# Seven block products in place of eight for some row-block pairs, in chunk pairs, with the heads first, in a one-core encoder block

## The chip, the cores and the metric

The kernel runs on one core of a Trainium2 chip. The metric is the device time of one execution in microseconds. TensorE is called PE, VectorE DVE, ScalarE ACT, GpSimd POOL and SyncE SP, as the profile calls them.

## What is computed

One layer of a hybrid encoder block on 256 tokens of width 2048, all in float32. `D_FF` is 5632; there are 8 retention heads with 256 columns of q and k and 512 of v and g each.

```python
h = rms_norm(x, g_mix)
cb, cc, cv, q, k, v, g, gate_conv, gate_ret = split(h @ w_in)          # 22528 columns
y_conv = (cb * causal_dwconv3(cc * cv)) @ w_conv_out
o = head_group_norm(retention(rotary(q), rotary(k), v), g_ret)
y_ret = (silu(g) * o) @ w_ret_out                                      # 4096 rows
x = x + (sigmoid(gate_conv) * y_conv + sigmoid(gate_ret) * y_ret) @ w_o
a, b = split(rms_norm(x, g_ffn) @ w_ffn_in)                            # 2 x 5632 columns
x = x + (silu(a) * b) @ w_ffn_out
x = x + sigmoid(rms_norm(x, g_ple) @ w_ple_gate) * (p @ w_ple_proj)
out = rms_norm(x, g_final)
```

## The kernel before

Every product of activations and weights goes through `project` (L204). Its output is one chunk of 512 columns (`W`) for the two token tiles of 128 rows, one PSUM bank each. The weights of a chunk are loaded in pieces of four row blocks of 128 rows (`KG`, 1 MB, four `raw` buffers, queue of SP). The float32 product is made of three products of fp32r parts: `split` (L184) copies two row blocks, 1024 columns, to the high part on ACT (L191) and subtracts on DVE to the low part (L192); `products` (L195) then issues, for each row block and token tile, high by high (L200), low weights by high (L201) and high weights by low (L202). The low and high parts of weights have three buffers each (`split_pool`). A row block thus costs 2 x 3 matmuls with 128x128 stationary and 512 moving columns, a chunk of 16 row blocks 96.

The activations stand transposed, features on partitions, as pairs of high and low parts: `transposed_split` (L145) turns a chunk by eight PE transposes (L137) into PSUM, from where ACT (L152 or, with a gain, L159) and DVE (L153 or L160) take the parts. Such steps are put off by `later` (L99) until so many `group_done` (L102) have passed, that is, pieces of four row blocks of the stream.

The order is: cc, cv, cb chunk by chunk with the short convolution (`conv_u`, `conv_gate`), then gc, gr and the convolution's output `co`, then the eight heads (qk, v, g each), the retention's output `ro`, `wo`, the feed-forward chunks fa and fb in turn, `fo` over all 44 row blocks, and the embedding with the last norm (pg, pp). The results of a chunk are read by ACT or DVE straight from PSUM. `project` has a pool of four banks (`ps_mm`), transposes, scores and the heads' outputs another of four (`ps_aux`). The instructions stand on each engine in an order that the tile scheduler sets when the program is built; each engine works through its own queue in that order, and an instruction that waits holds all behind it.

## Time and profile before

| | us |
|---|---|
| median of 3 runs | 2219.84 |
| lowest and highest | 2218.95, 2222.67 |
| span of the profiled execution | 2220.6 |
| PE busy, share of the span | 2205.8, 99% |
| DVE busy | 1222.5, 55% |
| ACT busy | 975.4, 44% |
| DMA queue q1, share of 16 engines | 55.2% |

The page gives no time of its own for the profiled execution beside its span, which lies 0.8 us above the median; so the sums below are made against 2220.6. A matmul's duration in a row (389 ns) is longer than its share of PE's time, since the matmuls are pipelined: the pace is read from the distance of their starts. A mean duration on DVE or ACT likewise overlaps the next operation by a little.

### The profile page before, as it was taken

The page shows a single profiled execution, that of the slowest core. Times are in us where ns is not written, and L with a number is a line of the kernel's source. Part 1 is how long each engine was busy: PE and PEld are TensorE (multiplying, and loading weights), DVE is VectorE, ACT ScalarE, POOL GpSimd, SP SyncE. Part 2 cuts the span into 40 slices and gives each one's busy share as a digit, 9 for nine tenths or more (in the row PEclk, how much of TensorE's full clock was granted, in tenths as well). Part 3 has the DMA queues.
Part 4 walks back from the last instruction along what each step waited for, and adds up shares of the span by engine and source line. Part 5 has one row for each costly group of instructions (what it writes and reads, how often), then busy time and mean ns, then how long its engine had stood idle before and what let it go on. Part 6 is the DMA issues. An engine that isn't in the chain of part 4 may idle for free.

```text
span 2220.6 us, 24771 instructions
## 1 busy us (share of the span) xinstructions
PE 2205.8 (99%) x10054; PEld 1834.0 (83%) x10054; DVE 1222.5 (55%) x1347; ACT 975.4 (44%) x1101; POOL 9.4 (0%) x19
## 2 busy tenths in 40 slices
...
GB/s 263 187 189 190 189 189 190 195 199 193 174 190 182 181 179 186 178 178 180 177 190 189 190 209 205 185 190 192 191 184 191 191 190 183 196 194 191 191 195 128
DMA packets 229106, 420.05 MB, mean 189 GB/s; under 512 B 7424, under 2 KB 42368, under 8 KB 228992
## 3 DMA queue, kind: packets, MB, share of 16 engines
q1 hardware_dynamic: 228992, 418.48, 55.2%
q8 instruction: 78, 1.28, 0.2%
...
## 4 chain that ended last, share of the span: by engine, by line
PE 99%; DMA 0%; ACT 0%; issue 0%; DVE 0%; SPq 0%; ACTq 0%; POOLq 0%
PE fo_ps L201 4%; PE fa_ps L202 4%; PE fa_ps L201 4%; PE fa_ps L200 4%; PE fo_ps L202 4%; PE fb_ps L200 4%; PE fo_ps L200 4%; PE fb_ps L202 4%; PE fb_ps L201 4%; PE v_ps L202 3%; PE v_ps L201 3%; PE v_ps L200 3%; PE g_ps L202 3%; PE g_ps L201 3%; PE g_ps L200 3%; PE qk_ps L201 3%
## 5 line engine op out<-in xcount | busy, mean ns | idle before, releaser
L192 DVE TENSOR_TENSOR fo_lo<-fo_raw,fo_hi 128x1024 fp32r<-128x1024 f32 x88 | 107.8, 1225 | 123.5 <-ACT fo_hi L191 123.5
L192 DVE TENSOR_TENSOR fa_lo<-fa_raw,fa_hi 128x1024 fp32r<-128x1024 f32 x88 | 107.8, 1225 | 111.4 <-ACT fa_hi L191 111.4
L192 DVE TENSOR_TENSOR fb_lo<-fb_raw,fb_hi 128x1024 fp32r<-128x1024 f32 x88 | 107.8, 1225 | 110.8 <-ACT fb_hi L191 110.8
L191 ACT CAST fa_hi<-fa_raw 128x1024 fp32r<-128x1024 f32 x88 | 92.8, 1054 | 142.8 <-PE fa_ps L202 87.9
L191 ACT CAST fo_hi<-fo_raw 128x1024 fp32r<-128x1024 f32 x88 | 92.8, 1055 | 137.4 <-PE fo_ps L202 132.4
L191 ACT CAST fb_hi<-fb_raw 128x1024 fp32r<-128x1024 f32 x88 | 92.7, 1053 | 121.9 <-PE fb_ps L202 85.3
L201 PE MATMUL fo_ps<-fo_lo,aT_hi 128*128 128x512 f32 x352 | 137.1, 389 | 0.0
L202 PE MATMUL fa_ps<-fa_hi,h2T_lo 128*128 128x512 f32 x352 | 137.0, 389 | 0.0
L201 PE MATMUL fa_ps<-fa_lo,h2T_hi 128*128 128x512 f32 x352 | 137.0, 389 | 0.0
L202 PE MATMUL fo_ps<-fo_hi,aT_lo 128*128 128x512 f32 x352 | 137.0, 389 | 0.0
L201 PE MATMUL fb_ps<-fb_lo,h2T_hi 128*128 128x512 f32 x352 | 136.9, 389 | 0.0
L202 PE MATMUL fb_ps<-fb_hi,h2T_lo 128*128 128x512 f32 x352 | 136.9, 389 | 0.0
L200 PE MATMUL fa_ps<-fa_hi,h2T_hi 128*128 128x512 f32 x352 | 127.2, 392 | 0.0
L200 PE MATMUL fo_ps<-fo_hi,aT_hi 128*128 128x512 f32 x352 | 124.4, 390 | 0.0
L192 DVE TENSOR_TENSOR ro_lo<-ro_raw,ro_hi 128x1024 fp32r<-128x1024 f32 x64 | 78.4, 1225 | 83.0 <-ACT ro_hi L191 83.0
L200 PE MATMUL fb_ps<-fb_hi,h2T_hi 128*128 128x512 f32 x352 | 122.6, 389 | 0.0
L191 ACT CAST g_hi<-g_raw 128x1024 fp32r<-128x1024 f32 x64 | 67.2, 1050 | 109.8 <-PE g_ps L202 81.9
L191 ACT CAST v_hi<-v_raw 128x1024 fp32r<-128x1024 f32 x64 | 67.4, 1054 | 106.3 <-PE v_ps L202 53.3
L192 DVE TENSOR_TENSOR v_lo<-v_raw,v_hi 128x1024 fp32r<-128x1024 f32 x64 | 78.3, 1224 | 62.4 <-ACT v_hi L191 62.4
L191 ACT CAST ro_hi<-ro_raw 128x1024 fp32r<-128x1024 f32 x64 | 67.5, 1054 | 102.3 <-PE ro_ps L202 98.9
L192 DVE TENSOR_TENSOR qk_lo<-qk_raw,qk_hi 128x1024 fp32r<-128x1024 f32 x64 | 78.3, 1224 | 61.0 <-ACT qk_hi L191 61.0
L192 DVE TENSOR_TENSOR g_lo<-g_raw,g_hi 128x1024 fp32r<-128x1024 f32 x64 | 78.3, 1224 | 60.4 <-ACT g_hi L191 60.4
...
## 6 DMA issues: line engine op xcount, KB each, us to landing
fa_raw<-in_w_ffn_in_dram SPq DMA_DIRECT2D x44, 1024.0 KB, 4.9
fb_raw<-in_w_ffn_in_dram SPq DMA_DIRECT2D x44, 1024.0 KB, 4.9
fo_raw<-in_w_ffn_out_dram SPq DMA_DIRECT2D x44, 1024.0 KB, 5.0
...
v_raw<-in_w_in_dram SPq DMA_DIRECT2D x32, 1024.0 KB, 5.0
g_raw<-in_w_in_dram SPq DMA_DIRECT2D x32, 1024.0 KB, 4.8
ro_raw<-in_w_ret_out_dram SPq DMA_DIRECT2D x32, 1024.0 KB, 5.0
cv_raw<-in_w_in_dram SPq DMA_DIRECT2D x16, 1024.0 KB, 4.9
```

What stands on the lines that cost most here:

```text
L191: last_copy[0] = nc.scalar.copy(out=hi, in_=raw[:, h0 : h0 + 2, :])
L192: nc.vector.tensor_tensor(out=lo, in0=raw[:, h0 : h0 + 2, :], in1=hi.bitcast(F32), op=ALU.subtract)
L200: nc.tensor.matmul(out=ps, lhsT=xh[:, ts], rhs=wh, start=first, stop=False)
L201: nc.tensor.matmul(out=ps, lhsT=xh[:, ts], rhs=wl, start=False, stop=False)
L202: nc.tensor.matmul(out=ps, lhsT=xl[:, ts], rhs=wh, start=False, stop=last)
```

## The change

Outside the heads, the retention's output and the embedding, chunks go in pairs. `product_group` takes two chunks of 512 columns at once, and row blocks in pairs, so that a step is a product of 2 x 2 blocks: two token tiles by two row blocks, and two row blocks by two chunks. Where the table `FAST3` or `FAST4` has True for a row-block pair (three or four of eight), the step has seven block products in place of eight, from sums and differences of the blocks: of the activations, made once by `further_forms` on DVE and ACT, and of the weights, made for each step by four DVE operations of 512 columns on the loaded piece (L260 to L263 of the changed kernel), after the parts of three of the four loaded blocks were taken and before the parts of the four combinations are. The products are accumulated in seven, at the end four, PSUM banks, and put together by one ACT copy and four DVE additions after the last such pair (L288 to L292) and four additions at the end (L297). The other pairs keep eight products, in a form that fits these sums.

`halves` replaces `split`: one ACT copy and one DVE subtraction over up to 2048 columns. One pool, `part`, of six buffers holds these parts, two buffers at each call; `raw` has three buffers, and one pool of eight PSUM banks serves all. `blk` has 30 in place of 36 buffers. Five heads come first, then the first half of the retention's output, which is put into DRAM (`acc`), the other three heads, the convolution with the second half of the retention's output after its first chunk, the gates, `co`, `wo`, and the feed-forward: after each chunk `f` from the third on, parts of the output product `fo` over two chunks' rows follow. In a head, g comes before qk and v.

```diff
...
+NBLK = 30
+FAST3 = (False, True, False, True, False, True, False, False)
+FAST4 = (False, True, False, True, True, False, True, False)
...
-    blk_pool = ctx.enter_context(tc.tile_pool(name="blk", bufs=36))
-    raw_pool = ctx.enter_context(tc.tile_pool(name="raw", bufs=4))
-    split_pool = ctx.enter_context(tc.tile_pool(name="split", bufs=3))
     small = ctx.enter_context(tc.tile_pool(name="small", bufs=2))
-    ps_mm = ctx.enter_context(tc.tile_pool(name="ps_mm", bufs=4, space=PSUM))
-    ps_aux = ctx.enter_context(tc.tile_pool(name="ps_aux", bufs=4, space=PSUM))
+    blk_pool = ctx.enter_context(tc.tile_pool(name="blk", bufs=NBLK))
+    diff_pool = ctx.enter_context(tc.tile_pool(name="diff", bufs=4))
+    raw_pool = ctx.enter_context(tc.tile_pool(name="raw", bufs=3))
+    part_pool = ctx.enter_context(tc.tile_pool(name="part", bufs=6))
+    ps_pool = ctx.enter_context(tc.tile_pool(name="ps", bufs=8, space=PSUM))
+    dram_pool = ctx.enter_context(tc.tile_pool(name="dram", bufs=1, space=bass.MemoryType.DRAM))
...
+    t1, t2 = slice(0, P), slice(P, 2 * P)
+    def further_forms(hi, lo, forms, fast, name):
+        stt = nc.vector.scalar_tensor_tensor
+        tt = nc.vector.tensor_tensor
+        for j0 in range(0, hi.shape[1], 2):
+            i = len(forms)
+            if not any(fast[i:]):
+                forms.append(None)
+                continue
+            js = slice(j0, j0 + 2)
+            a = small.tile([P, 2, S], F32, tag="form_a", name=f"{name}_a", bufs=1)
+            tt(out=a, in0=hi[:, js, :].bitcast(F32), in1=lo[:, js, :].bitcast(F32), op=ALU.add)
+            n = 4 if fast[i] else 2
+            mix = small.tile([P, 4, P], F32, tag="form_m", name=f"{name}_m", bufs=1)[:, :n, :]
+            if fast[i]:
+                a11, a12, a21, a22 = a[:, 0, t1], a[:, 1, t1], a[:, 0, t2], a[:, 1, t2]
+                stt(out=mix[:, 0, :], in0=a21, scalar=-1.0, in1=a22, op0=ALU.mult, op1=ALU.subtract)
+                stt(out=mix[:, 1, :], in0=mix[:, 0, :], scalar=-1.0, in1=a11, op0=ALU.mult, op1=ALU.subtract)
+                tt(out=mix[:, 2, :], in0=a11, in1=a21, op=ALU.subtract)
+                tt(out=mix[:, 3, :], in0=a12, in1=mix[:, 1, :], op=ALU.subtract)
+                more = blk([P, 2, 4, P], F32R, f"{name}_s")
+            else:
+                tt(out=mix, in0=a[:, :, t1], in1=a[:, :, t2], op=ALU.subtract)
+                more = diff_pool.tile([P, 2, 2, P], F32R, tag="diff", name=f"{name}_d")
+            nc.scalar.copy(out=more[:, 0], in_=mix)
+            tt(out=more[:, 1], in0=mix, in1=more[:, 0].bitcast(F32), op=ALU.subtract)
+            forms.append([(more[:, 0, k, :], more[:, 1, k, :]) for k in range(n)])
...
+    def product_group(lhs, forms, fast, w, c1, c2, name):
+        last_fast = max(i for i, f in enumerate(fast) if f)
+        left = {p: 0 for p in range(1, 9)}
+        for i, f in enumerate(fast):
+            for p in (1, 2, 3, 4, 5, 6, 7) if f else (2, 4, 3, 5) if i < last_fast else (2, 4, 3, 8):
+                left[p] += 1 if f else 2
+        total, banks = dict(left), {}
+        def add(p, stat, mov):
+            if p not in banks:
+                banks[p] = bank(f"{name}_p{p}")
+            thrice(banks[p], stat, mov, left[p] == total[p], left[p] == 1)
+            left[p] -= 1
+        tt = nc.vector.tensor_tensor
+        ca = blk([P, NT, W], F32, f"{name}_ca")
+        cb = blk([P, NT, W], F32, f"{name}_cb")
+        for i, f in enumerate(fast):
+            rows = w[2 * i * P : 2 * (i + 1) * P, :].rearrange("(c p) n -> p c n", p=P)
+            raw = raw_pool.tile([P, 4, W], F32, tag="raw", name=f"{name}_raw{i}")
+            nc.sync.dma_start(out=raw[:, 1:3, :], in_=rows[:, :, c1 : c1 + W])
+            nc.sync.dma_start(out=raw[:, 0:4:3, :], in_=rows[:, :, c2 : c2 + W])
+            blocks = lhs[2 * i : 2 * i + 2]
+            (a11, a21), (a12, a22) = ([(h[:, t], l[:, t]) for t in (t1, t2)] for h, l in blocks)
+            if f:
+                b11, b21, b22 = halves(raw[:, 1:4, :], f"{name}_b{i}")
+                tt(out=raw[:, 1, :], in0=raw[:, 1, :], in1=raw[:, 0, :], op=ALU.subtract)
+                tt(out=raw[:, 0, :], in0=raw[:, 3, :], in1=raw[:, 0, :], op=ALU.subtract)
+                tt(out=raw[:, 3, :], in0=raw[:, 3, :], in1=raw[:, 1, :], op=ALU.add)
+                tt(out=raw[:, 2, :], in0=raw[:, 2, :], in1=raw[:, 3, :], op=ALU.subtract)
+                t3, tt1, t4, tt2 = halves(raw, f"{name}_t{i}")
+                s1, s2, s3, s4 = forms[i]
+                for p, stat, mov in (
+                    (1, a11, b11),
+                    (2, a12, b21),
+                    (3, s4, b22),
+                    (7, s3, t3),
+                    (6, s2, tt2),
+                    (5, s1, tt1),
+                    (4, a22, t4),
+                ):
+                    add(p, stat, mov)
+            else:
+                b12, b11, b21, b22 = halves(raw, f"{name}_b{i}")
+                for j, (x1, x2, b1, b2) in enumerate(((a11, a21, b11, b12), (a12, a22, b21, b22))):
+                    add(2, x1, b1)
+                    add(4, x2, b1)
+                    if i < last_fast:
+                        add(5, x2, b2)
+                        add(3, forms[i][j], b2)
+                    else:
+                        add(3, x1, b2)
+                        add(8, x2, b2)
+            if i == last_fast:
+                nc.scalar.copy(out=ca[:, 0, :], in_=banks[1])
+                tt(out=cb[:, 0, :], in0=banks[6], in1=ca[:, 0, :], op=ALU.add)
+                tt(out=ca[:, 1, :], in0=banks[7], in1=cb[:, 0, :], op=ALU.add)
+                tt(out=cb[:, 1, :], in0=banks[5], in1=ca[:, 1, :], op=ALU.add)
+                tt(out=cb[:, 0, :], in0=banks[5], in1=cb[:, 0, :], op=ALU.add)
+            if i < len(fast) - 1:
+                group_done()
+        for p, c, t in ((2, ca, 0), (4, ca, 1), (3, cb, 0), (8, cb, 1)):
+            if p in banks:
+                tt(out=c[:, t, :], in0=banks[p], in1=c[:, t, :], op=ALU.add)
+        group_done()
+        return ca, cb
...
+    def halves(src, name):
+        n = src.shape[1]
+        hi, lo = (part_pool.tile([P, 4, W], F32R, tag="part", name=f"{name}_{x}") for x in ("hi", "lo"))
+        last_copy[0] = nc.scalar.copy(out=hi[:, :n, :], in_=src)
+        nc.vector.tensor_tensor(out=lo[:, :n, :], in0=src, in1=hi[:, :n, :].bitcast(F32), op=ALU.subtract)
+        return [(hi[:, j, :], lo[:, j, :]) for j in range(n)]
...
+    head(0, first)
+    for h in range(1, HEADS // 2):
+        head(h)
+    head(4)
+    ret_out(0)
+    for h in range(5, HEADS):
+        head(h, gate_last=h == HEADS - 1)
...
+    def conv_cv(n):
+        c, v = product_group(hT, hF, FAST3, w_in[0], C_C + n * W, C_V + n * W, f"cv{n}")
         for t in range(NT):
+            nc.scalar.activation(out=c[:, t, :], in_=c[:, t, :], func=AF.Copy, scale=r1[t])
             nc.vector.scalar_tensor_tensor(
+                out=v[:, t, :], in0=v[:, t, :], scalar=r1[t], in1=c[:, t, :], op0=ALU.mult, op1=ALU.mult
             )
+        uT = small.tile([P, 4, S + 2], F32, tag="uT", name=f"uT{n}", bufs=1)
+        ys[n] = blk([P, 4, S], F32, f"y{n}")
+        later(2, partial(conv_u, n, v, uT, ys[n]))
+    def conv_b(n):
+        bs = product_group(hT, hF, FAST3, w_in[0], C_B + n * W, C_B + (n + 1) * W, f"cb{n}")
+        for i, b in enumerate(bs):
+            for t in range(NT):
+                nc.scalar.activation(out=b[:, t, :], in_=b[:, t, :], func=AF.Copy, scale=r1[t])
+            later(2 + i, partial(conv_gate, n + i, b, ys[n + i]))
+    conv_cv(0)
+    ret_out(1)
+    conv_cv(1)
+    conv_b(0)
+    conv_cv(2)
+    conv_cv(3)
+    conv_b(2)
...
+    for n in range(0, D // W, 2):
+        ms = product_group(ycT, ycF, FAST3, w_conv_out[0], n * W, (n + 1) * W, f"co{n}")
+        for i, m in enumerate(ms):
+            gc, gr = gates[n + i]
+            nc.vector.tensor_tensor(out=m, in0=m, in1=gc, op=ALU.mult)
+            nc.vector.tensor_tensor(out=m, in0=m, in1=gr, op=ALU.add)
+            later(2 + i, partial(turn_m, n + i, m))
...
+    def ffn_in(n):
+        a, b = product_group(h2T, h2F, FAST4, w_ffn_in[0], n * W, D_FF + n * W, f"f{n}")
+        r2 = scale2[0] = scale2[0] or rows2.done()
         sa = blk([P, NT, W], F32, f"sa{n}")
         for t in range(NT):
+            nc.scalar.activation(out=sa[:, t, :], in_=a[:, t, :], func=AF.Sigmoid, scale=r2[t])
             nc.vector.scalar_tensor_tensor(
+                out=a[:, t, :], in0=a[:, t, :], scalar=r2[t], in1=sa[:, t, :], op0=ALU.mult, op1=ALU.mult
             )
+            nc.vector.scalar_tensor_tensor(
+                out=a[:, t, :], in0=b[:, t, :], scalar=r2[t], in1=a[:, t, :], op0=ALU.mult, op1=ALU.mult
+            )
+        later(2, partial(turn_a, n, a))
...
+    for n in range(NF):
+        ffn_in(n)
+        if n >= 2:
+            part = (n // 2 - 1) * 2
+            for c in (0, 1) if n % 2 == 0 and n < NF - 1 else (2, 3) if n % 2 else ():
+                ffn_out((part, part + 1), c)
+    for c in range(D // W):
+        ffn_out((NF - 3, NF - 2, NF - 1), c, last=True)
...
```

The first place is DVE's queue in the feed-forward, at chunk 5. Before, in chunk fb5, each row is the low part of two row blocks, with two products of the chunk fa5 between:

```order
L192 TENSOR_TENSOR fb5_lo0_11559<-fb5_raw_11556,fb5_hi0_11558 128x1024
L192 TENSOR_TENSOR fb5_lo2_11563<-fb5_raw_11556,fb5_hi2_11562 128x1024
L554 SCALAR_TENSOR_TENSOR sa5_11549<-fa5_ps0_11395,r2_r_9219,sa5_11549 128x512
L554 SCALAR_TENSOR_TENSOR sa5_11549<-fa5_ps1_11396,r2_r_9219,sa5_11549 128x512
L192 TENSOR_TENSOR fb5_lo0_11593<-fb5_raw_11590,fb5_hi0_11592 128x1024
L192 TENSOR_TENSOR fb5_lo2_11597<-fb5_raw_11590,fb5_hi2_11596 128x1024
L192 TENSOR_TENSOR fb5_lo0_11627<-fb5_raw_11624,fb5_hi0_11626 128x1024
L192 TENSOR_TENSOR fb5_lo2_11631<-fb5_raw_11624,fb5_hi2_11630 128x1024
```

Now, at the row-block pairs 3 and 4 of chunk f5, both with seven products (`b` are parts of loaded blocks, `t` parts of combinations):

```order
L329 TENSOR_TENSOR f5_b3_lo_11783<-f5_raw3_11779,f5_b3_hi_11782 128x1536
L260 TENSOR_TENSOR f5_raw3_11779<-f5_raw3_11779 128x512
L261 TENSOR_TENSOR f5_raw3_11779<-f5_raw3_11779 128x512
L262 TENSOR_TENSOR f5_raw3_11779<-f5_raw3_11779 128x512
L263 TENSOR_TENSOR f5_raw3_11779<-f5_raw3_11779 128x512
L329 TENSOR_TENSOR f5_t3_lo_11791<-f5_raw3_11779,f5_t3_hi_11790 128x2048
L329 TENSOR_TENSOR f5_b4_lo_11819<-f5_raw4_11815,f5_b4_hi_11818 128x1536
L260 TENSOR_TENSOR f5_raw4_11815<-f5_raw4_11815 128x512
L261 TENSOR_TENSOR f5_raw4_11815<-f5_raw4_11815 128x512
L262 TENSOR_TENSOR f5_raw4_11815<-f5_raw4_11815 128x512
L263 TENSOR_TENSOR f5_raw4_11815<-f5_raw4_11815 128x512
L329 TENSOR_TENSOR f5_t4_lo_11827<-f5_raw4_11815,f5_t4_hi_11826 128x2048
```

Between the low part `b3_lo` and the low part `t3_lo` now stand four operations on the loaded piece, each of which waits for DVE's own count, and the next pair's `b4_lo` comes only after `t3_lo`. On ACT's queue the copies stand in the order `b3_hi`, `t3_hi`, `b4_hi`, `t4_hi`: `t3_hi` reads the piece `f5_raw3` that the four operations wrote, and `b4_hi` stands behind it.

The second place is PE's queue at the same chunk. Before, for one row block of fb5, three products for each token tile:

```order
L200 MATMUL fb5_ps0_11554<-fb5_hi0_11558,h2T0_hi_9417 128x512
L201 MATMUL fb5_ps0_11554<-fb5_lo0_11559,h2T0_hi_9417 128x512
L202 MATMUL fb5_ps0_11554<-fb5_hi0_11558,h2T0_lo_9418 128x512
L200 MATMUL fb5_ps1_11555<-fb5_hi0_11558,h2T0_hi_9417 128x512
L201 MATMUL fb5_ps1_11555<-fb5_lo0_11559,h2T0_hi_9417 128x512
L202 MATMUL fb5_ps1_11555<-fb5_hi0_11558,h2T0_lo_9418 128x512
```

And now, from the products with `t3` to the first with `b4`'s low part:

```order
L227 MATMUL f5_p7_11734<-f5_t3_hi_11790,h2T1_s_9461 128x512
L227 MATMUL f5_p6_11738<-f5_t3_hi_11790,h2T1_s_9461 128x512
L227 MATMUL f5_p5_11689<-f5_t3_hi_11790,h2T1_s_9461 128x512
L227 MATMUL f5_p4_11685<-f5_t3_hi_11790,h2T1_hi_9427 128x512
L227 MATMUL f5_p1_11724<-f5_b4_hi_11818,h2T2_hi_9727 128x512
L227 MATMUL f5_p2_11681<-f5_b4_hi_11818,h2T2_hi_9727 128x512
L227 MATMUL f5_p3_11693<-f5_b4_hi_11818,h2T2_s_9754 128x512
L228 MATMUL f5_p7_11734<-f5_t3_lo_11791,h2T1_s_9461 128x512
L229 MATMUL f5_p7_11734<-f5_t3_hi_11790,h2T1_s_9461 128x512
L228 MATMUL f5_p6_11738<-f5_t3_lo_11791,h2T1_s_9461 128x512
L229 MATMUL f5_p6_11738<-f5_t3_hi_11790,h2T1_s_9461 128x512
L228 MATMUL f5_p5_11689<-f5_t3_lo_11791,h2T1_s_9461 128x512
```

Four products with `t3_hi` and three with `b4_hi` stand ahead of those that need `t3_lo`; all of b4's others stand behind these. The third place is DVE's queue in the convolution. Before, the taps of chunk 1 (`y1`, L326 and L331) stood between two low parts:

```order
L192 TENSOR_TENSOR cb1_lo0_1092<-cb1_raw_1089,cb1_hi0_1091 128x1024
L326 TENSOR_SCALAR y1_993<-uT1_992,gains_76 128x256 x4
L331 SCALAR_TENSOR_TENSOR y1_993<-uT1_992,gains_76,y1_993 128x256 x6
L192 TENSOR_TENSOR cb1_lo2_1096<-cb1_raw_1089,cb1_hi2_1095 128x1024
L331 SCALAR_TENSOR_TENSOR y1_993<-uT1_992,gains_76,y1_993 128x256 x2
L192 TENSOR_TENSOR cb1_lo0_1126<-cb1_raw_1123,cb1_hi0_1125 128x1024
```

Now the taps (L649) stand between the four operations on the piece `cb0_raw3`:

```order
L329 TENSOR_TENSOR cb0_b3_lo_5936<-cb0_raw3_5932,cb0_b3_hi_5935 128x1536
L649 SCALAR_TENSOR_TENSOR y1_5799<-uT1_5798,gains_78,y1_5799 128x256 x2
L260 TENSOR_TENSOR cb0_raw3_5932<-cb0_raw3_5932 128x512
L649 SCALAR_TENSOR_TENSOR y1_5799<-uT1_5798,gains_78,y1_5799 128x256 x4
L261 TENSOR_TENSOR cb0_raw3_5932<-cb0_raw3_5932 128x512
L649 SCALAR_TENSOR_TENSOR y1_5799<-uT1_5798,gains_78,y1_5799 128x256 x2
L262 TENSOR_TENSOR cb0_raw3_5932<-cb0_raw3_5932 128x512
L640 MEMSET uT2_6433 128x4x2
L263 TENSOR_TENSOR cb0_raw3_5932<-cb0_raw3_5932 128x512
L329 TENSOR_TENSOR cb0_t3_lo_5944<-cb0_raw3_5932,cb0_t3_hi_5943 128x2048
L329 TENSOR_TENSOR cb0_b4_lo_5972<-cb0_raw4_5968,cb0_b4_hi_5971 128x2048
```

There other work separates the four operations, and none stands between L263 and `cb0_t3_lo`.

In the whole program PE has 10054 matmuls before and 9796 after, DVE 1347 and 1707 instructions, ACT 1066 and 842. In 16 of the 86 steps with seven products something else stands on DVE's queue between L263 and the low part of the combinations, in 70 nothing.

## Rows read from the trace of the kernel before

**Rows 1.** The page: span, busy time of each engine, and the chain that ended last.

```profile
span 2220.6 us, 24771 instructions
PE 2205.8 (99%) x10054; PEld 1834.0 (83%) x10054; DVE 1222.5 (55%) x1347; ACT 975.4 (44%) x1101; POOL 9.4 (0%) x19
PE 99%; DMA 0%; ACT 0%; issue 0%; DVE 0%; SPq 0%; ACTq 0%; POOLq 0%
```

**Rows 2.** Windows of convolution, heads, feed-forward: length, PE, PEld, DVE, ACT, POOL, PEclk, DMA, GB/s.

```profile
60.00:545.00 485.00, 485.00 (x2173) 402.27 (x2172) 249.39 (x257) 212.46 (x222) 0.00 (x0) 1.00 0.56 191
545.00:1129.00 584.00, 584.00 (x2679) 484.75 (x2678) 366.47 (x464) 254.93 (x287) 5.52 (x8) 1.00 0.54 181
1390.00:1870.00 480.00, 480.00 (x2160) 398.34 (x2159) 254.62 (x238) 205.91 (x215) 0.00 (x0) 1.00 0.55 189
```

**Rows 3.** Chain in order of time (start, length, engine): transposes, and matmuls 96 apart.

```profile
64.73 0.87 PE uT L137 x8
436.38 0.45 PE gr_ps L200 x2
458.13 0.45 PE co_ps L200 x2
```

**Rows 4.** Groups by line and shape, DVE: busy us, mean ns, idle before and releaser.

```profile
L192 DVE TENSOR_TENSOR fa_lo<-fa_raw,fa_hi 128x1024 fp32r<-128x1024 f32 x88 | 107.8, 1225 | 111.4 <-ACT fa_hi L191 111.4
L331 DVE SCALAR_TENSOR_TENSOR y<-uT,gains,y 128x256 f32<-128x256 f32 x32 | 13.3, 479 | 0.0
L520 DVE TENSOR_TENSOR m<-m,co 128x512 f32<-128x512 f32 x8 | 5.1, 682 | 0.0
L160 DVE SCALAR_TENSOR_TENSOR h2T_lo<-h2T_t,gains,h2T_hi 128x256 fp32r<-128x256 f32 x16 | 7.0, 478 | 0.6 <-ACT h2T_hi L159 0.2
L589 DVE TENSOR_TENSOR x<-x,x 128x256 f32<-128x256 f32 x4 | 1.7, 425 | 0.1
```

**Rows 5.** Timeline of DVE, independent operations back to back: start, length.

```profile
1154.72 1.28 DVE L519 TENSOR_TENSOR m<-ro_ps,gr 128x512 f32<-128x512 f32 x2
1155.92 1.28 DVE L520 TENSOR_TENSOR m<-m,co 128x512 f32<-128x512 f32 x2
1157.12 1.22 DVE L192 TENSOR_TENSOR ro_lo<-ro_raw,ro_hi 128x1024 fp32r<-128x1024 f32 x1
```

**Rows 6.** Timeline of DVE, operations that read what the one before wrote (L589 after L588).

```profile
2199.52 0.42 DVE L588 TENSOR_TENSOR x<-pp_ps,x 128x256 f32<-128x256 f32 x1 [3.10 <-ACT x L587]
2199.98 0.42 DVE L589 TENSOR_TENSOR x<-x,x 128x256 f32<-128x256 f32 x1
2200.32 0.42 DVE L588 TENSOR_TENSOR x<-pp_ps,x 128x256 f32<-128x256 f32 x1
```

**Rows 7.** Groups by line and shape, ACT: the same columns as rows 4.

```profile
L191 ACT CAST fa_hi<-fa_raw 128x1024 fp32r<-128x1024 f32 x88 | 92.8, 1054 | 142.8 <-PE fa_ps L202 87.9 <-PE fb_ps L202 50.0 <-PE wo_ps L202 4.9
L347 ACT CAST ych<-y 128x512 fp32r<-128x512 f32 x8 | 4.9, 622 | 0.4
```

**Rows 8.** Timeline, from ACT's copy to the DVE operation that waits for it.

```profile
1501.42 1.05 ACT L191 CAST fb_hi<-fb_raw 128x1024 fp32r<-128x1024 f32 x1 [1.67 <-PE fb_ps L202]
1502.51 1.22 DVE L192 TENSOR_TENSOR fb_lo<-fb_raw,fb_hi 128x1024 fp32r<-128x1024 f32 x1 [1.49 <-ACT fb_hi L191]
```

**Rows 9.** Waits of PE: engine, line, waited for; us, times, longest.

```profile
PE cc_ps L200 <- ACT hT_hi L159: 4.2, 1, 4.2
```

**Rows 10.** Windows at the start, columns as in rows 2: TensorE's clock around that wait.

```profile
4.00:8.00 4.00, 2.15 (x14) 1.63 (x12) 0.17 (x1) 0.00 (x0) 0.00 (x0) 1.00 0.90 295
8.00:12.00 4.00, 1.68 (x4) 1.21 (x5) 2.08 (x4) 3.14 (x6) 0.00 (x0) 0.52 1.02 373
12.00:16.00 4.00, 4.00 (x16) 3.43 (x16) 2.73 (x5) 2.27 (x6) 0.00 (x0) 0.62 1.05 392
16.00:20.00 4.00, 4.00 (x19) 3.27 (x19) 3.22 (x5) 2.48 (x4) 0.00 (x0) 1.00 1.03 378
```

**Rows 11.** The page's DMA issues (KB each, us to landing) and the queue's share.

```profile
q1 hardware_dynamic: 228992, 418.48, 55.2%
fa_raw<-in_w_ffn_in_dram SPq DMA_DIRECT2D x44, 1024.0 KB, 4.9
```

305 lines of the change are left out of this document (168 added, 137 removed).

## The prediction

> **What bounds the kernel now.** I read the page's shares and its chain first: PE is busy for 99% of the span and the whole chain is PE, while DVE has 55% and ACT 44% [rows 1]. An average can hide a stage, so the windows come next: in the convolution, the heads and the feed-forward PE is busy in every microsecond at full clock, and DVE has 249 of 485, 366 of 584 and 255 of 480 us [rows 2]. The kernel is a PE stream from end to end. Its pace is read from the chain: two first matmuls of pieces that lie 96 matmuls apart start at 436.38 and 458.13, so one costs 21.75 / 96 = 0.2266 us; eight transposes cost 0.87 [rows 3]. The DMA queue is at 55%, and a piece of 1 MB lands in 4.9 us [rows 11]; both kernels load the same weights, and a `raw` buffer comes free whole pairs (5 us each) before it is needed, so I put no cost on transfers. PE waits only once for ACT, for 4.2 us at the start [rows 9].
>
> **What is taken from PE.** A step with seven products drops one of eight block products, three matmuls. The FAST3 groups are 14 (4 cv, 2 cb, 4 gate, 2 co, 2 wo) with 3 such steps, the FAST4 groups 11 with 4: 42 + 44 = 86 steps, 258 matmuls, as the order counts (10054 to 9796). At 0.2266 that is 58.5 us. If PE stayed the bound, the time would be 2162 us. So all depends on whether DVE and ACT can feed it.
>
> **What one step costs on DVE.** Durations of shapes that the trace lacks come from its shapes: on DVE 1024 elements take 1225 ns and 512 take 682 [rows 4], 1.06 ns per element, so I estimate 1.77 us for 1536 and 2.31 for 2048. Independent operations start 0.08 before the one before ends (pairs of 512 at 1154.72, 1155.92, 1157.12, so 0.60 each) [rows 5], so a 2048 one occupies 2.23. Operations that wait for the one before start 0.04 after its end (0.46 from start to start for 0.42 of work, against 0.34 without the wait) [rows 6], so each of the four operations L260 to L263, which all wait for DVE's own count, takes 0.68 + 0.04 = 0.72; the lower bound is 0.60. On ACT 1024 take 1054 ns and 512 take 622 [rows 7], 0.844 ns per element, so a 2048 copy takes 1.92; from its end to the DVE operation that needs it pass 0.04 [rows 8].
>
> The order has DVE do, for one such step, `b_lo` (1.77 + 0.04), the four operations (2.88), then `t_lo`, which waits for ACT's copy `t_hi`, which waits for L263. In 70 of 86 steps nothing stands between, so DVE stands still for 0.04 + 1.92 + 0.04 = 2.0 us; then `t_lo` 2.23. Sum 8.92 us. PE has for the same step 21 x 0.2266 = 4.76 us. An ordinary step is the reverse: DVE 2.23, PE 24 x 0.2266 = 5.44. The closing eight additions of a group (L289 to L297) are 8 x about 0.64 = 5.1 us more on DVE. `b_hi` of the next step stands behind `t_hi` on ACT, and `b_lo` behind `t_lo` on DVE, so no buffer can shorten this: DVE's queue runs step after step, and PE can only use up what was made ahead.
>
> **Stages with FAST3.** DVE per group: 3 x 8.92 + 5 x 2.23 + 5.1 = 43.0. PE: 183 matmuls, 41.5; before, 2 x 21.75 = 43.5. So DVE already passes PE, and all other work on DVE falls on the path. I count it by the operations, with 0.40 for 256 elements, 0.60 to 0.68 for 512 and 1.14 for two of 512 less the overlap [rows 4, 5]: the forms of the activations (13 with seven products at 0.68 + 4 x 0.33 + 0.68 = 2.7, 12 others at 0.68 + 2 x 0.4 = 1.45) 52; L682 8 x 0.67 = 5; taps 32 x 0.40 = 13; L664 and L666 16 x 0.60 = 10; the products with the gates 16 x 1.14 = 18; low parts of mT and h2T 8 x 0.60 and 16 x 0.42 = 12; what head 7 leaves, 9. That is 119. Off it go 20, for the 16 standstills in which such work lies (1.3 each), and 10 beside the second half of the retention's output, where all steps are ordinary and DVE has time to spare. The stage comes to 14 x 43.0 + 119 - 30 = 691. Before, the same products and 16 sets of transposes took 28 x 21.75 + 16 x 0.87 = 623. **Cost 68 us.**
>
> **The feed-forward.** From the third chunk on, two parts of `fo` (96 ordinary matmuls) follow each group. PE's time for such a period is (180 + 96) x 0.2266 + 0.87 = 63.4, DVE's 4 x 8.92 + 4 x 2.23 + 5.1 + 3.9 for the products with r2 and aT + 4 x 2.23 for `fo` = 62.5. They are even, so what counts is the order within the period: steps 3 and 4 are neighbours and take 2 x (8.92 - 4.76) = 8.3 more of DVE than of PE, while what is made ahead of them in six buffers is one step, about 4.7: PE stands for about 3.7 there, and for 1.45 at step 6 (4.2 less the 2.7 won in step 5). Period 68.5; before 288 x 0.2266 + 0.87 = 66.1; over 9 periods +22. The first two chunks have no `fo` behind: DVE 4 x 8.92 + 4 x 2.23 + 5.1 + 3.9 = 53.6, before 43.5 + 0.87 = 44.4, so 9.2 x 2 = +18. **Cost 40 us.**
>
> **What costs nothing.** Heads, retention output and embedding keep 24 matmuls for 2.23 of DVE per two row blocks, and DVE had 366 of 584 us in the heads [rows 2]; the merged copies leave that sum as it was (two of 1225 against one of 2.31) and the different order of heads and convolution moves PE work only. The trips of the retention sum through DRAM are a few pieces among 218 MB and are not read until stages later. Sum: 2220.6 + 68 + 40 = 2328.6, set against the span 2220.6, 0.8 above the median; I say **2328**.
>
> **A rule against the merging.** The row shows a 1024 copy on ACT at 1.05 and the DVE operation behind it 0.04 later [rows 7, 8]; with 2048 elements the first DVE operation can't start before all four blocks are copied. The Trainium skill, "Perfetto Trace Analysis", section Optimizing Scalar/DVE Operations, advises to break up instructions that cause bubbles on other engines. By it, halves would make the standstill about 1.1 instead of 2.0 and the sum some 86 x 0.9 = 77 us smaller at most; the kernel does the opposite, so my sum keeps the 2.0.
>
> **Rivals.**
> *A, faster: PE stays the bound.* With s for DVE's time per step, the FAST3 stage takes 14 x (3 x s + 16.3) + 89 us (11.2 and 5.1 in each group, 119 - 30 beside), as long as this is over PE's 595. At s = 7.3 it is 623, what it was, and the feed-forward then has about 20 us of PE's gain: 2200. Without the standstill s is 6.92, the stage 607, the time about 2175; at 6.6 all is PE's, 2162. For it: DVE's busy time after, 1222 + 86 x 4.4 (a 1536 low part and four operations, less the merging) + 25 x 5.1 + 60 of forms, is about 1790 of 2162 us, under PE's; and where DVE is ahead its standstill hides. Against it: 2.0 of the 8.92 is a wait whose two ends the order shows, and in the FAST3 groups there is no slack to be ahead with. The skill page named, section Identifying the Most-Contended Engine, takes the engine with the highest occupancy as the bottleneck; by that PE still is, and the time 2162. In the trace of before the rule held [rows 1]. Chance 0.10.
>
> *B, far slower: the clock falls.* After PE's one wait the granted clock was 0.52 and 0.62 over 8 us, which is the 1.2 GHz level for most of them, and 1.00 again from 16 us on [rows 10]. If the waits of 1.5 to 4 us in the groups did the same, the 1.2 GHz level over 4 to 8 us, that is 3 to 6 us more in each of 25 groups, would put 75 to 150 on top: 2405 to 2480. Against it: most stalls here are split over a step, PE working between. Chance 0.09.
>
> *C, near no change, 2216 to 2250:* s between 7.7 and 8.1, as with the four operations at 0.60 (s = 8.44) and some of the standstills filled besides. Chance 0.05, of which 0.03 within 0.2%.
>
> *That it doesn't do what it says* is excluded by the count of matmuls in the order.
>
> **The range.** Low: four operations at 0.60 give 86 x 4 x 0.12 = -41; the stalls of the feed-forward taken up by the reserve give -25; holes filled, -12: 2250. High: the PE transposes, which stand in PE's queue and wait for DVE's sums of the group before, at 1.5 us in 25 groups, +38; short falls of the clock [rows 10], +40: 2405. Within lies 0.76, the rest being A, B and C. About 0.2% is what measurement can tell from no change here; faster by more than it has 0.10, within it 0.03, slower 0.87.
>
> **What would show it.** Right: DVE waits for ACT at the line of `t_lo`, about 2 us each, 70 times or more; PE waits for parts of weights, its share falls to about 92% with the chain passing through DVE and ACT; FAST3 groups last 47 to 50 us, feed-forward periods about 68, the first two chunks about 53; DVE is busy about 1790 us. Wrong: PE at 98% and more without such waits (A); L260 to L263 clearly under 0.68 apart; PEclk under 1.00 over whole stages (B); or PE waiting for DMA, which my sum has at nothing.

## The result, and the profile after

The changed kernel takes 2330.26 us (median of 4 runs, 2326.76 to 2332.11) against 2219.39 before: a ratio of 1.0491, 95% interval 1.0477 to 1.0506. It is slower, by 111 us, and 2 us from the time that was forecast. The page of the profiled execution, three lines that answer to [rows 1]:

```profile
span 2329.7 us, 24877 instructions
PE 2214.4 (95%) x9796; PEld 1803.6 (77%) x9796; DVE 1710.1 (73%) x1707; ACT 1048.8 (45%) x877; POOL 10.2 (0%) x19
PE 67%; DVE 17%; ACT 6%; issue 5%; DMA 3%; SPq 0%; ACTq 0%; DVEq 0%; POOLq 0%
```

PE lost its 258 matmuls and is busy for 9 us more than before; the chain, all PE before, now goes through DVE and ACT for 23%. Windows by stage show where (columns as in [rows 2]): cv of chunk 0; the second half of the retention's output (from 721.5 to 809.5); the rest of the stages with FAST3; the feed-forward.

```profile
669.20:718.00 48.80, 43.30 (x177) 33.50 (x176) 40.84 (x48) 23.85 (x23) 0.00 (x0) 0.93 0.43 148
718.00:810.50 92.50, 92.50 (x414) 76.69 (x413) 50.96 (x42) 35.27 (x25) 0.00 (x0) 1.00 0.69 231
810.50:1434.40 623.90, 578.00 (x2481) 457.97 (x2479) 532.10 (x543) 306.36 (x252) 0.00 (x0) 0.98 0.54 183
1434.40:2220.20 785.80, 738.53 (x3168) 597.51 (x3169) 633.86 (x599) 359.05 (x276) 1.47 (x1) 0.96 0.52 177
```

Apart from the start and the end, only the stages with seven products have a PE that is not busy all the time, and in the last two of these windows DVE has 85% and 81%. Measured from the first matmul of a stage to the first of the next, and without the 87.9 us of the retention's output between: the stages with FAST3 take 677 us where the same products took 625; the feed-forward 786 where it took 732; heads, retention output and start 757 for 754; the embedding 109.5 for 109.7. The loss is 52 + 54 + 3.5.

What DVE waits for, of the rows with a `t_lo` (us in all, times, longest):

```profile
DVE f_t_lo L329 <- ACT f_t_hi L328: 85.6, 42, 2.1
DVE gate_t_lo L329 <- ACT gate_t_hi L328: 19.9, 10, 2.6
DVE cv_t_lo L329 <- ACT cv_t_hi L328: 19.2, 10, 2.1
DVE cb_t_lo L329 <- ACT cb_t_hi L328: 12.1, 6, 2.1
DVE wo_t_lo L329 <- ACT wo_t_hi L328: 11.0, 5, 3.4
DVE co_t_lo L329 <- ACT co_t_hi L328: 8.5, 5, 2.1
```

78 waits of 2.0 us, 156 us in all. In the stages with FAST3 these are 71 us beside 573 of DVE's busy time, of 673 us; in the feed-forward 86 beside 634, of 786. So a DVE that is busy for 81% to 85% has a queue with little room left. And what PE waits for, which answers to [rows 9], the first rows:

```profile
PE f_p L227 <- ACT f_t_hi L328: 38.1, 15, 3.4
PE cv_p L227 <- ACT cv_t_hi L328: 8.1, 5, 3.2
PE co_p L227 <- ACT co_t_hi L328: 6.6, 4, 2.9
```

One step with seven products on DVE, pair 3 of a chunk f and the beginning of pair 4 (timeline: start, length; in brackets idle time and releaser):

```profile
1698.86 1.75 DVE L329 TENSOR_TENSOR f_b_lo<-f_raw,f_b_hi 128x1536 fp32r<-128x1536 f32 x1
1700.65 0.69 DVE L260 TENSOR_TENSOR f_raw<-f_raw 128x512 f32<-128x512 f32 x1
1701.37 0.69 DVE L261 TENSOR_TENSOR f_raw<-f_raw 128x512 f32<-128x512 f32 x1
1702.10 0.69 DVE L262 TENSOR_TENSOR f_raw<-f_raw 128x512 f32<-128x512 f32 x1
1702.82 0.69 DVE L263 TENSOR_TENSOR f_raw<-f_raw 128x512 f32<-128x512 f32 x1
1705.57 2.29 DVE L329 TENSOR_TENSOR f_t_lo<-f_raw,f_t_hi 128x2048 fp32r<-128x2048 f32 x1 [2.05 <-ACT f_t_hi L328]
1707.78 1.75 DVE L329 TENSOR_TENSOR f_b_lo<-f_raw,f_b_hi 128x1536 fp32r<-128x1536 f32 x1
```

From `b_lo` to `b_lo` are 8.92 us, the four operations start 0.72 apart, the standstill is 2.05: the term on which the prediction's sum rests, to the hundredth. PE meets it one step later:

```profile
1711.46 0.39 PE L229 MATMUL f_p<-f_b_hi,h2T_s 128*128 128x512 f32 x1
1714.50 1.65 PE L227 MATMUL f_p<-f_t_hi,h2T_s 128*128 128x512 f32 x3 [2.65 <-ACT f_t_hi L328]
1715.94 0.63 PE L227 MATMUL f_p<-f_t_hi,h2T_hi 128*128 128x512 f32 x1
1716.37 0.73 PE L227 MATMUL f_p<-f_b_hi,h2T_hi 128*128 128x512 f32 x1
1718.21 0.40 PE L229 MATMUL f_p<-f_t_hi,h2T_s 128*128 128x512 f32 x1
```

It stands for 2.65 us, and the matmuls behind take 0.63 in place of 0.39, for some 3 us: the granted clock has fallen (0.83 in the windows under "Zeros in the stall").

### The profile page after: what moved, and what is told of

The parts are those of the page before. It is cut to its first block, busy times and chain, and to the rows that moved or that the text cites. A ratio compares the mean times of both kernels' runs of the same rounds, so it can differ in the third digit from the quotient of the medians.

```text
span 2329.7 us, 24877 instructions
## 1 busy us (share of the span) xinstructions
PE 2214.4 (95%) x9796; PEld 1803.6 (77%) x9796; DVE 1710.1 (73%) x1707; ACT 1048.8 (45%) x877; POOL 10.2 (0%) x19
## 3 DMA queue, kind: packets, MB, share of 16 engines
q1 hardware_dynamic: 235008, 426.88, 54.4%
## 4 chain that ended last, share of the span: by engine, by line
PE 67%; DVE 17%; ACT 6%; issue 5%; DMA 3%; SPq 0%; ACTq 0%; DVEq 0%; POOLq 0%
PE f_p L227 3%; PE f_p L228 3%; PE f_p L229 3%; PE fo_ps L350 3%; PE fo_ps L348 3%; PE fo_ps L349 3%; PE g_ps L348 3%; PE g_ps L349 3%; PE g_ps L350 3%; DVE f_b_lo L329 3%; PE v_ps L350 2%; PE ro_ps L229 2%; PE ro_ps L228 2%; PE qk_ps L350 2%; PE qk_ps L348 2%
## 5 line engine op out<-in xcount | busy, mean ns | idle before, releaser
L329 DVE TENSOR_TENSOR f_b_lo<-f_raw,f_b_hi 128x2048 fp32r<-128x2048 f32 (+1 forms) x88 | 176.1, 2020 | 20.8 <-ACT f_b_hi L328 20.6
L328 ACT CAST f_b_hi<-f_raw 128x2048 fp32r<-128x2048 f32 (+1 forms) x88 | 147.6, 1692 | 54.4 <-PE fo_ps L349 27.3
L329 DVE TENSOR_TENSOR f_t_lo<-f_raw,f_t_hi 128x2048 fp32r<-128x2048 f32 x44 | 100.9, 2292 | 85.6 <-ACT f_t_hi L328 85.6
L228 PE MATMUL f_p<-f_b_lo,h2T_hi 128*128 128x512 f32 x374 | 146.0, 390 | 0.0
L229 PE MATMUL f_p<-f_b_hi,h2T_lo 128*128 128x512 f32 x374 | 145.6, 389 | 0.0
L227 PE MATMUL f_p<-f_b_hi,h2T_hi 128*128 128x512 f32 x374 | 138.3, 407 | 6.3 <-ACT f_b_hi L328 4.6
L329 DVE TENSOR_TENSOR fo_lo<-fo_raw,fo_hi 128x2048 fp32r<-128x2048 f32 x44 | 100.5, 2284 | 17.3 <-ACT fo_hi L328 17.2
L348 PE MATMUL g_ps<-g_hi,hT_hi 128*128 128x512 f32 x256 | 100.7, 395 | 6.0 <-ACT g_hi L328 6.0
L349 PE MATMUL g_ps<-g_lo,hT_hi 128*128 128x512 f32 x256 | 100.8, 394 | 0.0
L348 PE MATMUL v_ps<-v_hi,hT_hi 128*128 128x512 f32 x256 | 100.4, 392 | 0.0
```

Of the source, the lines that this page charges most:

```text
L227: nc.tensor.matmul(out=ps, lhsT=xh, rhs=wh, start=first, stop=False)
L228: nc.tensor.matmul(out=ps, lhsT=xh, rhs=wl, start=False, stop=False)
L229: nc.tensor.matmul(out=ps, lhsT=xl, rhs=wh, start=False, stop=last)
L328: last_copy[0] = nc.scalar.copy(out=hi[:, :n, :], in_=src)
L329: nc.vector.tensor_tensor(out=lo[:, :n, :], in0=src, in1=hi[:, :n, :].bitcast(F32), op=ALU.subtract)
L348: nc.tensor.matmul(out=ps, lhsT=xh[:, ts], rhs=wh, start=first, stop=False)
```

## The experiments

The theory: DVE's queue, step by step and with its standstill, sets the time in groups with seven products as far as its sum passes PE's. The rivals: the rest of the rewrite costs; banks, additions and forms cost; the clock costs. The table has every run; "mix" are the stages with FAST3 without the 87.9 us, "ffn" the feed-forward, both from first matmul to first matmul in the trace, in us. Each ratio is to runs of the kernel before that were made together with that run (their medians lie between 2219.4 and 2222.7), so it can differ by some 0.15% from the quotient of the medians shown. The expectations that speak of 672 us and of a loss of 47 for "mix" leave out 92.5 us around the retention's output in place of 87.9; they mean the 677 and the 52 of here.

| kernel | median | ratio to before (95%) | mix | ffn |
|---|---|---|---|---|
| before | 2219.4 | | 625 | 732 |
| changed | 2330.3 | 1.0491 (1.0477 to 1.0506) | 677 | 786 |
| eight products everywhere | 2223.1 | 1.0004 (0.9994 to 1.0013) | 622 | 733 |
| without the four operations | 2178.6 | 0.9805 (0.9790 to 0.9819) | 603 | 707 |
| halves | 2248.3 | 1.0118 (1.0101 to 1.0135) | 638 | 742 |
| FAST4 apart | 2295.7 | 1.0330 (1.0315 to 1.0345) | 677 | 752 |
| zeros | 2327.4 | 1.0470 (1.0455 to 1.0485) | 677 | 783 |
| halves, apart | 2232.0 | 1.0043 (1.0027 to 1.0059) | 635 | 730 |
| halves, apart, FAST3 two | 2211.3 | 0.9948 (0.9934 to 0.9962) | 615 | 728 |
| halves, apart, FAST3 none | 2217.9 | 0.9980 (0.9970 to 0.9989) | 622 | 730 |
| FAST3 two | 2281.2 | 1.0272 (1.0255 to 1.0289) | 623 | 791 |
| halves, FAST3 two, FAST4 three | 2216.3 | 0.9980 (0.9969 to 0.9991) | 617 | 730 |
| halves, apart, FAST3 two, forms on GpSimd | 2212.0 | 0.9956 (0.9942 to 0.9971) | 614 | 730 |
| FAST4 none | 2271.6 | 1.0223 (1.0206 to 1.0240) | 673 | 733 |

### Eight products everywhere

```diff
-FAST3 = (False, True, False, True, False, True, False, False)
-FAST4 = (False, True, False, True, True, False, True, False)
+FAST3 = (False,) * 8
+FAST4 = (False,) * 8
-        last_fast = max(i for i, f in enumerate(fast) if f)
+        last_fast = max((i for i, f in enumerate(fast) if f), default=-1)
...
-            if p in banks:
+            if p in banks and last_fast < 0:
+                nc.vector.tensor_copy(c[:, t, :], banks[p])
+            elif p in banks:
```

> The changed kernel with eight products in every step: both tables hold False only, and the sums of a group are copied out of their four banks. Pairs of chunks, merged parts, pools and the order of the stages stay. Theory (DVE's queue in the steps with seven products makes the loss): PE has the matmuls of before and is fed by 2.3 us of DVE per 5.4 of its own, so the time is that of before or some us over it, 2215 to 2240, with PE at 98% or more. Rival (the rest of the rewrite costs: one pool of banks, three raw buffers, merged copies, heads first): 2260 or more, with PE waiting for copies or DMA.

It took 2223.1, within its interval the time of before, and its page is that of before:

```profile
span 2221.2 us, 24459 instructions
PE 2205.6 (99%) x10054; PEld 1835.8 (83%) x10054; DVE 1246.5 (56%) x1063; ACT 907.2 (41%) x741; POOL 9.4 (0%) x19
```

Pairs of chunks, merged copies, three raw buffers, one pool of banks and the new order of stages together cost nothing that can be measured. The first rival is gone; the whole loss hangs on the steps with seven products.

### Without the four operations

```diff
-                tt(out=raw[:, 1, :], in0=raw[:, 1, :], in1=raw[:, 0, :], op=ALU.subtract)
-                tt(out=raw[:, 0, :], in0=raw[:, 3, :], in1=raw[:, 0, :], op=ALU.subtract)
-                tt(out=raw[:, 3, :], in0=raw[:, 3, :], in1=raw[:, 1, :], op=ALU.add)
-                tt(out=raw[:, 2, :], in0=raw[:, 2, :], in1=raw[:, 3, :], op=ALU.subtract)
```

> The changed kernel without the four DVE operations on the loaded piece (L260 to L263): the seven products are made with the parts of the plain blocks, so the sums of blocks are left out of the computation. PE's work, the copies, the low parts, the closing additions and the forms of the activations stay. Theory: without them nothing makes the copy t_hi wait, DVE's step is 1.8 + 2.3 = 4.1 us beside PE's 4.8, and PE is the bound again: 2165 to 2190. Rival (banks, closing additions, forms or DMA hold PE up): 2250 or more.

2178.6, faster than before by about 2%, with the second parts, the closing additions, the seven banks and the forms all in place:

```profile
span 2176.6 us, 24622 instructions
PE 2152.0 (99%) x9796; PEld 1784.3 (82%) x9796; DVE 1490.7 (68%) x1363; ACT 1055.4 (48%) x877; POOL 9.4 (0%) x19
```

So 152 us of the changed kernel's time come from 344 operations whose own time is 344 x 0.69 = 237 us, and from what waits for them. Banks, additions and forms hold PE up by no more than the 15 us between this span, 2176.6, and 2162.

### Halves

```diff
-    def halves(src, name):
+    def halves(src, name, step=4):
...
-        last_copy[0] = nc.scalar.copy(out=hi[:, :n, :], in_=src)
-        nc.vector.tensor_tensor(out=lo[:, :n, :], in0=src, in1=hi[:, :n, :].bitcast(F32), op=ALU.subtract)
+        for a in range(0, n, step):
+            js = slice(a, min(a + step, n))
+            last_copy[0] = nc.scalar.copy(out=hi[:, js, :], in_=src[:, js, :])
+            nc.vector.tensor_tensor(out=lo[:, js, :], in0=src[:, js, :], in1=hi[:, js, :].bitcast(F32), op=ALU.subtract)
...
-                t3, tt1, t4, tt2 = halves(raw, f"{name}_t{i}")
+                t3, tt1, t4, tt2 = halves(raw, f"{name}_t{i}", 2)
```

> The changed kernel with the parts of the combinations made in two halves of 1024 columns, copy and low part each: the first half holds the results of L260 and L261, so its copy (1.05 us) can run beside L262 and L263, and the second copy beside the first low part. DVE's work stays, its standstill of 2.0 us in front of t_lo should go. Theory: DVE's step falls from 8.9 to about 7.1 us, 86 x 1.8 = 155 us at most, of which PE's own bound leaves 120 to 140: 2185 to 2230. Rival (the four operations and additions alone hold PE, the standstill is hidden by parts made ahead): 2300 to 2335. Rival (more instructions cost as much as the standstill): 2320 or more.

Same work, 82 us less than the changed kernel: 2248.3. The timeline of DVE, and below it that of ACT, at pair 3 of a chunk f:

```profile
1642.67 0.69 DVE L260 TENSOR_TENSOR f_raw<-f_raw 128x512 f32<-128x512 f32 x1
1643.39 0.69 DVE L261 TENSOR_TENSOR f_raw<-f_raw 128x512 f32<-128x512 f32 x1
1644.12 0.69 DVE L262 TENSOR_TENSOR f_raw<-f_raw 128x512 f32<-128x512 f32 x1
1644.85 0.69 DVE L263 TENSOR_TENSOR f_raw<-f_raw 128x512 f32<-128x512 f32 x1
1645.46 2.43 DVE L331 TENSOR_TENSOR f_t_lo<-f_raw,f_t_hi 128x1024 fp32r<-128x1024 f32 x2
1648.67 1.76 DVE L331 TENSOR_TENSOR f_b_lo<-f_raw,f_b_hi 128x1536 fp32r<-128x1536 f32 x1 [0.78 <-ACT f_b_hi L330]
1650.46 0.69 DVE L260 TENSOR_TENSOR f_raw<-f_raw 128x512 f32<-128x512 f32 x1
```

```profile
1644.20 1.05 ACT L330 CAST f_t_hi<-f_raw 128x1024 fp32r<-128x1024 f32 x1 [3.94 <-DVE f_raw L261]
1645.58 1.05 ACT L330 CAST f_t_hi<-f_raw 128x1024 fp32r<-128x1024 f32 x1 [0.33 <-DVE f_raw L263]
1647.15 1.48 ACT L330 CAST f_b_hi<-f_raw 128x1536 fp32r<-128x1536 f32 x1 [0.52 <-PE f_p L228]
```

The first copy starts when L261 is done and runs beside L262 and L263; DVE goes on without a gap into the low part of the combinations. So the standstill was on the path, as the prediction had it; here the Trainium skill's advice ("Perfetto Trace Analysis", section Optimizing Scalar/DVE Operations: break up instructions that cause bubbles on other engines) agrees with the run. But the expectation of 2185 to 2230 was missed by 18 us: the gain is 82, not 120 to 140. A part of the waiting came back one operation later: DVE's waits in front of `b_lo`, before and with the halves, and those left in front of `t_lo`:

```profile
DVE f_b_lo L329 <- ACT f_b_hi L328: 20.6, 25, 2.9
DVE f_b_lo L331 <- ACT f_b_hi L330: 61.3, 49, 3.5
DVE f_t_lo L331 <- ACT f_t_hi L330: 16.0, 19, 1.3
```

Of the 85.6 us in front of `t_lo` in the feed-forward 69.6 went, and 40.7 came back in front of `b_lo`. In the timeline a step, from L260 to L260, is 7.79 us where the expectation had about 7.1: the copy `b_hi` has waited 0.52 for PE, which by the order of the pool `part` had still to read the buffer that it takes. With PE's sum near DVE's (in the stages with FAST3 595 us, and 607 by the prediction's formula with 6.9 us per step, where 638 were measured), each waits for the other in turn, PE in short waits, DVE for copies that wait for free buffers.

### FAST4 apart, and both together

```diff
-FAST4 = (False, True, False, True, True, False, True, False)
+FAST4 = (True, False, True, False, True, False, True, False)
```

> The changed kernel with FAST4's four steps of seven products at pairs 0, 2, 4 and 6, so that no two are neighbours. The work is the same. Theory of the prediction (neighbouring steps outrun what is made ahead): the feed-forward's stalls at the fourth step and the clock's falls behind them go, 2 to 4 us in each of 11 groups: 2290 to 2315. Rival (DVE's sum over the period decides, wherever the steps stand): 2325 to 2335.

2295.7: of the feed-forward's 54 us of loss, 34 go by the place of the steps alone. Its periods, read at the ACT copy of bank p1, fall from 69.1 to 65.5 us, PE's own being 63.4. With the halves as well:

> The halves of the combinations' parts, as in the run with halves alone (2248), together with FAST4's four steps at pairs 0, 2, 4 and 6. Theory (in the feed-forward what remains of the stalls comes from the neighbours): the feed-forward goes from 742 us to 705 to 720, its PE time being 702: 2210 to 2228. Rival (DVE's sum in the groups with FAST3 and in the closing additions is all that remains): 2240 to 2250.

2232.0, 4 us over the range: the feed-forward falls by 12 us, not by 22 to 37. Its periods now are 63.5, at PE's pace; what is left of the loss lies in the first three chunks, which have no product `fo` among them.

### Zeros in the stall

```diff
+    zero = const.tile([P, 32], F32R, name="zero")
+    nc.scalar.activation(out=zero, in_=ident[:, :32], func=AF.Copy, scale=0.0)
...
+                    if p == 7 and fast is FAST4 and i == 4:
+                        for _ in range(10):
+                            nc.tensor.matmul(out=banks[1][:32, :], lhsT=zero, rhs=b11[0], start=False, stop=False)
                     add(p, stat, mov)
```

> The changed kernel with ten matmuls more (a stationary of zeros on the parts of b4, added to bank p1) ahead of the products with t4 in each of the 11 chunks f, that is in PE's longest stall of a feed-forward group (2.65 us in chunk f5). 110 matmuls are 24.9 us of PE's time, put where it waits anyhow. Theory (the stall also lowers the clock behind it, and this costs beside the wait): the stall is filled, the clock stays at 1.00 there, and the time falls by 10 to 30 us in spite of more work: 2300 to 2320. Rival (the wait alone costs, and the low clock behind it runs in time that DVE's queue would take anyhow): 2327 to 2340. Rival (the ten are not hidden): 2345 to 2356.

2327.4; the intervals of its ratio and the changed kernel's overlap. PE at the same place as in the timeline above, and windows of 5 us there, of the run and then of the changed kernel:

```profile
1712.32 2.48 PE L279 MATMUL f_p<-f_b_hi,zero 128*32 128x512 f32 x10
1715.14 0.97 PE L229 MATMUL f_p<-f_t_hi,h2T_s 128*128 128x512 f32 x3 [0.34 <-ACT f_t_hi L333]
```

```profile
1711.00:1716.00 5.00, 4.66 (x21) 2.66 (x19) 2.88 (x4) 2.81 (x2) 0.00 (x0) 1.00 0.35 135
1716.00:1721.00 5.00, 4.39 (x19) 3.22 (x18) 5.00 (x3) 2.27 (x2) 0.00 (x0) 1.00 0.48 159
```

```profile
1711.00:1716.00 5.00, 2.35 (x8) 1.53 (x6) 2.91 (x3) 3.45 (x2) 0.00 (x0) 0.83 0.26 101
1716.00:1721.00 5.00, 5.00 (x20) 3.84 (x19) 4.96 (x4) 1.62 (x2) 0.00 (x0) 0.83 0.61 201
```

The stall is filled, the clock stays at 1.00 where it was 0.83, PE does 110 matmuls (24.9 us) more, and the time is the same within a few us. The theory (2300 to 2320) fails and so does the second rival (2345 and more); the first holds, at its lower edge: the low clock ran in time that DVE's queue took anyhow, and PE is not the bound there. This is shown for the longest stall of the feed-forward's groups; no run fills the stalls of the stages with FAST3, where the granted clock was 0.98. PE's busy time is the highest of all engines in the changed kernel (95%), and yet work added in this stall is free. The Trainium skill's rule ("Perfetto Trace Analysis", section Identifying the Most-Contended Engine: the most-contended engine is the one with the highest occupancy, and TensorE's headroom is judged by MFU or by its weight loads) names PE in the changed kernel by both shares on its page of the profile (95%, weight loads 77%, against DVE's 73%). From that rule the prediction had 2162; here the measurement decides against it.

### Fewer steps

```diff
-FAST3 = (False, True, False, True, False, True, False, False)
+FAST3 = (False, True, False, False, True, False, False, False)
```

Alone, on the changed kernel:

> The changed kernel with two steps of seven products in FAST3 (pairs 1 and 4) in place of three; FAST4 and the parts in one piece stay. Theory (a threshold: PE loses time only by as much as DVE's sum in a group passes PE's): DVE per group falls by 8.9 - 2.2 = 6.7 us and PE's rises by 0.7; 672 us measured for the stage less 14 x 6.7 is 578, under PE's 605, so the stage goes nearly at PE's pace, 605 to 620: the whole 2263 to 2280. Rival (each step costs its own stall wherever the sum stands): a third of the 47 us goes, less 14 x 0.7 gained by PE's work: 2320 to 2330.

2281.2, a microsecond over the range, and the stages with FAST3 take 623 us: one step less of three takes away 54 us. That is the threshold of the theory; a loss by the step would have left 2320. But PE's pace, 605, is not reached: with two steps the stages take what eight products take (622). The closing additions come one pair earlier and fewer forms are made with two steps; the run doesn't separate this from the step itself. The feed-forward, left as it was, took 791 in place of 786. With the halves and FAST4 apart ("the run before" is the one of 2232.0):

> As the run before, with two steps of seven products in FAST3 (pairs 1 and 4) in place of three. DVE per group is 2 x 7.1 + 6 x 2.23 + 5.1 + 8.5 = 41.2 us, just under PE's 42.2: theory, the stage goes to PE's pace, 14 x 42.2 + 14 = 605 us from 633, and the whole to 2180 to 2205, faster than both kernels. Rival (stalls come from the place of closing additions and forms, not from DVE's sum): no gain against three steps.

2211.3, over the range by 6 us, but the fastest of all versions that leave nothing out, 0.5% faster than before. Its feed-forward, in windows of its beginning and of one period:

```profile
1371.90:1420.00 48.10, 41.91 (x172) 32.19 (x171) 46.02 (x67) 28.18 (x35) 0.69 (x1) 0.93 0.43 150
1420.00:1470.00 50.00, 46.96 (x203) 36.87 (x203) 46.40 (x48) 23.81 (x21) 0.00 (x0) 1.00 0.51 175
1580.10:1643.60 63.50, 63.50 (x286) 52.58 (x285) 56.61 (x54) 32.19 (x25) 0.00 (x0) 1.00 0.58 199
```

From the fourth chunk on PE is busy in every microsecond; the first three take 148 us for 124 of PE's work, with DVE busy for 96% in the first. Two runs went after these 24 us. Three steps in FAST4, at pairs 1, 3 and 6, so that number and place change together:

> Parts of the combinations in halves, FAST3 at pairs 1 and 4, FAST4 at three pairs (1, 3 and 6) in place of four. The three feed-forward groups with no product fo behind them lost some 24 us together in the run with four steps (148 us for 124 of PE). Theory: with three steps DVE's sum is under PE's there too, the 24 us go and 11 x 0.68 = 7.5 come back as matmuls: 2190 to 2200. Rival (the loss in these groups comes from the forms and the transposes of the stage's start): 2211 to 2219.

2216.3, a miss, and within the rival's range: the feed-forward stays at 730, and after the first chunk DVE now has idle time, waiting for copies that wait for a load or a free buffer. And the plain operations of the forms on GpSimd:

```diff
     def further_forms(hi, lo, forms, fast, name):
         stt = nc.vector.scalar_tensor_tensor
-        tt = nc.vector.tensor_tensor
+        tt = nc.gpsimd.tensor_tensor
```

> As the run with halves, FAST3 at pairs 1 and 4 and FAST4 at 0, 2, 4 and 6 (2211), with the plain additions and subtractions of the forms of the activations on GpSimd in place of DVE. Theory (DVE's queue at the start of the feed-forward is lengthened by the forms): some 10 of the 24 us lost there go: 2198 to 2206. Rival (GpSimd's operations take longer, or slow DVE down, and PE waits for the forms): 2211 or more.

2212.0, no change against DVE. But the run did not relieve DVE's queue: its rival, that GpSimd's operations slow DVE down, came. The beginning of the feed-forward with the forms on GpSimd, one form on GpSimd, and DVE at the same time:

```profile
1369.90:1420.00 50.10, 41.99 (x170) 31.78 (x170) 48.40 (x52) 28.30 (x35) 17.42 (x12) 0.90 0.39 132
1398.52 1.67 POOL L208 TENSOR_TENSOR h2T_a<-h2T_hi,h2T_lo 128x512 f32<-128x512 f32 x1 [2.09 <-DVE h2T_lo L172]
1398.36 0.68 DVE L260 TENSOR_TENSOR f_raw<-f_raw 128x512 f32<-128x512 f32 x1
1399.07 1.66 DVE L261 TENSOR_TENSOR f_raw<-f_raw 128x512 f32<-128x512 f32 x1
```

Beside GpSimd's operation L261 took 1.66 us on DVE where it takes 0.68 or 0.69 otherwise, and DVE, with 52 operations in place of 67, was still busy for 97% of the window. So the number of steps alone doesn't hold the beginning of the feed-forward; whether the forms do is not shown by this run, and the cause stays open.

### One stage at a time

> As the run with halves and FAST4 at pairs 0, 2, 4 and 6, with no step of seven products in FAST3. The stages up to wo go at PE's pace with eight products, 625 us; the feed-forward as in the run before. Theory: 2200 to 2215, so that what the two stages gain or lose simply adds. Rival (the feed-forward's gain depends on what the stages ahead leave): off that by over 10 us.

2217.9, 3 us over the range; the feed-forward is 730 as in the run with FAST3. And the changed kernel with FAST4 all False:

> The changed kernel with FAST4 all False: the feed-forward has eight products in every step, the stages with FAST3 are as in the changed kernel. Theory (the two stages' losses add; the trace of the changed kernel puts 47 us on FAST3's stages and 54 on the feed-forward): 2264 to 2276. The prediction's own term for FAST3 was 68, by which it would be about 2290. Rival (a part of the FAST3 stages' loss is passed on, and taken back, by the feed-forward): off by 10 us or more from 2270.

2271.6: 50 us over before, nearly all in the stages with FAST3 (673 for 625). The two stages' losses add.

## Why the prediction was right

**PE's side.** The 258 matmuls went, and where DVE feeds PE they are worth what was said: 2178.6 without the four operations, 2162 being the sum without any wait.

**DVE's step.** 8.92 us was forecast and 8.92 stands in the timeline; the estimates for shapes that [rows 4] and [rows 7] lack held (2.29 for 2.31, 1.75 for 1.77 on DVE, 1.91 for 1.92 on ACT). The four dependent operations took the upper of the two bounds, 0.72, as in [rows 6]. 78 standstills of 2.0 were seen where 70 whole and 16 shortened ones were expected. Of the signs that the prediction named, the waits, the stages' lengths and the chain through DVE and ACT came; PE's share did not fall to 92% but to 95%. The same 9796 matmuls kept PE busy for 2152.0 us in the run without the four operations, at a granted clock of 0.997, and for 2214.4 here, at 0.979.

**Stages with FAST3.** +68 forecast, +52 by the trace and +50 by the run with FAST4 all False. The term that was too large is the other work of 119 us. It counted all 25 forms of the activations into this stage; by the rows of the form's first addition (L208), three of hT's six were done during the heads and three of h2T's seven in the feed-forward. Six forms at some 2.1 us are 13 of the 16 us.

**The feed-forward.** +40 forecast, +54 measured. A period with `fo` takes 69.1 (68.5 forecast) and the chunks without it 54.4 (53.6). Half of the error is a miscount: of eleven chunks only eight have a product `fo` ahead of them, not nine, so three chunks lose 10 us and eight lose 3: 30 + 24. At the forecast's own 9.2 and 2.4 the right count would have given 47; the other 7 are chunks and periods that each took 0.6 to 0.8 us longer. The neighbours at pairs 3 and 4 were named as the reason for the periods, and setting them apart took 34 us away.

That the total came out within 2 us is thus partly luck: one stage was 16 us too dear, the other 14 too cheap, and 3.5 us at the start were put at nothing (PE's first wait is 6.0 us in place of 4.2, and the granted clock from 16 to 20 us is 0.76 in place of 1.00).

**The rivals.** A asked that the standstill be covered: with the halves most of it is, and 2248 came out where the formula gave 2175. The formula takes the larger of two sums and counts no wait beside the standstill; where the sums are within a few per cent, both engines wait in turn, and the waits in front of `b_lo` grew from 20.6 to 61.3 us. The prediction's own sum for the halves was 77 us at most; 82 came. B came true in the records (granted clock 0.979 over the span, 0.998 before) but, where it was tested, not in the time: the run with zeros brought the clock to 0.988, and its median is 3 us lower, with intervals that overlap. Its price was mis-sized too: half the clock over 4 to 8 us costs 2 to 4 us, not 3 to 6. The +40 that the range held for it was not needed. C did not come.

**The unneeded terms.** The PE transposes that were to wait for DVE's sums cost next to nothing: PE's waits at them are 0.2 to 2.9 us, 3.3 in all. DVE's busy time was 1710 us, not about 1790. Two slips changed little: an ordinary step leaves DVE 5.44 - 2.23 = 3.2 us ahead, not 2.7, and the loads are 418 MB [rows 11], not 218.
